# Pairing the last two gate blocks, requesting decay rows a step sooner, and taking group norm's roots on a whole row

## The chip, the cores and the metric

The kernel runs on one core of one Trainium2 chip. The metric is the device time of one execution in microseconds (us), as the median of the runs shown. A core has five engines that run side by side and wait for each other by semaphores: PE (TensorE, matrix products), DVE (VectorE), ACT (ScalarE), POOL (GpSimd) and SP (SyncE, which here only issues transfers). POOL also issues transfers, in the order of its own program.

## The reference

One decoder layer on 1024 tokens of width 1024. The part that matters here:

```python
hn = rms_norm(h, norm_mix_g)
za, zb, zc, xbc, dt_raw, g_raw = split(hn @ w_in)      # one projection feeds everything
ya = gmlp_mixer(za, ...)
yb = rg_lru_mixer(zb, ...)
yc = ssd_mixer(zc, xbc, dt_raw, ...)
gates = sigmoid(g_raw.reshape(..., 3, 1024) + b_gate)  # 24 blocks of 128 columns
merged = sum(gates[k] * (y_k @ w_branch_k) for k in range(3))
h = h + merged @ w_out
# ... then the MLP and a last norm

# inside ssd_mixer, in chunks of 128 tokens, 4 groups of 4 heads:
#   decay[l, s] = exp(acs[l] - acs[s])      (one row acs per chunk and head)
#   y = y_diag(decay) + exp(acs) * (C @ state) + x * d_skip
#   y = y * silu(z)
#   y = y * rsqrt(mean(y*y over the 256 columns of the group) + eps) * norm_g
```

## The kernel before, in words

Everything is computed in float32 split into a high and a low part, so that a product of two matrices is three products (high·high, high·low, low·high). Channels lie on the partitions and tokens on the columns.

**Units.** The projection is worked off in *units* of 128 output columns (`one_unit`, `product` L549): 48 matmuls (8 blocks of the inner dimension, 3 parts, 2 halves of 512 tokens) into one PSUM tile `ps` of 1024 columns. Two such tiles exist. After each unit its `post` function reads `ps`, and `step()` then lets every pending generator (`later(...)`) run to its next `yield`. So each `yield` is worth one unit of PE time, and a generator says in which unit's shadow its work is meant to lie. A scheduler then orders the instructions of each engine; every engine runs its own in order.

**The order of the units.** Four rounds, one for each SSD group g: b, c, x0, x1, z0, z1 (`ssd_units`), then two LRU heads with an x unit and a gate unit each (`lru_units`). Then eight GMLP units (`gmlp_unit`), then two single gate units (`gate_unit` L873, blocks 6 and 7 of branch 1), each a full unit of 48 matmuls. The other 22 gate blocks are computed after that as 11 *pairs* (`GatePair` L926): two blocks of 128 columns by 1024 tokens as a 2x2 block product with seven products in place of eight (`seventh` L472), each 12 matmuls of 512 columns, 84 for a pair. Pairs need sums of quarters of the normed input (`x_forms` L884: T1, T2, T4 and the third, written back over X at its end), which are prepared by steps under the GMLP units; the first pair's weights are prepared by `first_pair` (L978).

**The SSD stages** (`ssd_stages` L649) of a round have ten steps. The token halves 0 and 1 go through `rows_in` (L658, rows of the decays, 128 copies), `s1_` (L664, transposes, C·B products, decay matrices E), `s2_` (L697, chunk states `pv`), `s3_` (L722, y) , `roots_` (L743) and `s4_` (L749, norm and store). `s2_` begins with the requests for the tiles `er` (L701): four transfers on POOL's queue that copy rows of exp(acs) from DRAM to 64 partitions each. `s3_` multiplies by `er` on DVE (L735), straight out of the PSUM tiles `yo` that PE has just written, adds `yi` (L736), the skip (L737), and z (L738); then ACT squares (L740) and POOL adds the two squares (L741).

**The roots before.** `roots_` sums the squares over the partitions with four products by a single column of ones (L746), which leaves four columns of 128 numbers; `rsqrt_cols` (L115) takes the inverse roots of these four columns with three small DVE instructions and twelve small POOL instructions. `s4_` spreads them over the partitions with four products by the identity (L753) into a PSUM tile that two DVE instructions read (L756).

**Shared tiles.** PSUM tiles of 512 columns (`aux`, four of them) serve the transposes, C·B, chunk states, yo, yi, root sums and the LRU's gate products (L815). Tiles of 512 columns in SBUF (`half_`, sixteen) serve xdt, xw, pv, er, squares and the LRU's temporaries. A tile is given out anew when its last reader is done, so a late reader delays whatever takes the tile next.

**The order on POOL** is one queue for small arithmetic, for the transfers `wl` (L527, which make the low part of the next units' weights), for `yb_d`/`yc_d`/`ya_d` stores and for the requests of decay rows.

Of the kernel before, what the change touches and what calls it, by code (L numbers as in the profile page):

```python
# [8 lines left out]
F32 = mybir.dt.float32  # L9
# [3 lines left out]
ALU = mybir.AluOpType  # L13
# [23 lines left out]
def trunk_kernel(ctx: ExitStack, tc: tile.TileContext, x, norm_mix_g, w_in, b_gate, gmlp_ln_g, gmlp_ln_b,  # L37
# [37 lines left out]
    def half_(shape=(P, HF), dt=F32):  # L75
        return halfp.tile(list(shape), dt, tag="half", name=nm("h"))
# [208 lines left out]
    with tc.manual_schedule():  # L285
# [24 lines left out]
        nc.gpsimd.affine_select(out=tri, in_=ones, pattern=[[1, P]], compare_op=ALU.is_ge, fill=0.0,  # L310
                                base=0, channel_multiplier=-1)
        g2c = base.tile([P, 2 * KD], F32, name="g2c")
        groot = base.tile([P, 8], F32, name="groot")
        ss, rs = sm(NCH, "ss"), sm(NCH, "rsx")
        v2[NCH - 1] = act()

# [332 lines left out]
    def ssd_stages(g, S):  # L649
        Bf, Cf, Xf = S["b"], S["c"], (S["x0"], S["x1"])  # L650
        hs = slice(4 * g, 4 * g + 4)
        Bt = act((P, NCH, P))
        xdt, xw, E, cb, pv, er, sq = {}, {}, {}, {}, {}, {}, {}

        def tok(c):
            return slice(c * P, (c + 1) * P)

        def rows_in(half):  # L658
            for q in (2 * half, 2 * half + 1):
                e = E[q] = act((P, 2, 4, P))  # L660
                for cc in range(2):
                    nc.gpsimd.dma_start(out=e[:, cc], in_=acs_v[0, 2 * q + cc, hs, :].partition_broadcast(P))

        def s1_(half):  # L664
            for q in (2 * half, 2 * half + 1):
                ps = aux()
                for cc in range(2):
                    for j in range(2):
                        o = cc * 256 + j * P
                        nc.tensor.transpose(out=ps[:, o:o + P], in_=Xf[j][:, tok(2 * q + cc)], identity=ident)  # L670
                ev = ps.rearrange("p (c h d) -> p c h d", c=2, h=4)
                xdt[q], xw[q] = half_((P, 2, 4, 64)), half_((P, 2, 4, 64))
                tt(out=xdt[q], in0=ev, in1=dt[:, 2 * q:2 * q + 2, hs].unsqueeze(3).to_broadcast([P, 2, 4, 64]), op=ALU.mult)
                tt(out=xw[q], in0=ev, in1=w2[:, 2 * q:2 * q + 2, hs].unsqueeze(3).to_broadcast([P, 2, 4, 64]), op=ALU.mult)
            ps = aux()
            for i in range(4):
                nc.tensor.transpose(out=ps[:, tok(i)], in_=Bf[:, tok(half * 4 + i)], identity=ident)
            actv(Bt[:, half * 4:half * 4 + 4, :], ps.rearrange("p (c n) -> p c n", c=4), AF.Copy)
            cb[half] = aux()
            for i in range(4):  # L680
                c = half * 4 + i
                mm(cb[half][:, tok(i)], Bf[:, tok(c)], Cf[:, tok(c)], start=True, stop=True)

            cbm = half_((P, 4, P))
            tt(out=cbm, in0=cb[half].rearrange("p (c l) -> p c l", c=4), in1=tri.unsqueeze(1).to_broadcast([P, 4, P]), op=ALU.mult)
            for q in (2 * half, 2 * half + 1):
                e = E[q]
                for cc in range(2):
                    for h in range(4):
                        col = (2 * q + cc) * 16 + 4 * g + h  # L690
                        actv(e[:, cc, h, :], e[:, cc, h, :], AF.Relu, scale=-1.0, bias=acs[:, col:col + 1])
                actv(e, e, AF.Exp, scale=-1.0)
                for cc in range(2):
                    i = (2 * q + cc) % 4
                    tt(out=e[:, cc], in0=e[:, cc], in1=cbm[:, i].unsqueeze(1).to_broadcast([P, 4, P]), op=ALU.mult)

        def s2_(half):  # L697
            for j in range(2):
                t = er[half, j] = half_((P, 4, P))
                for h in range(2):  # L700
                    nc.gpsimd.dma_start(out=t[64 * h:64 * h + 64], in_=acs_v[1, half * 4:half * 4 + 4, 4 * g + 2 * j + h, :].partition_broadcast(64))  # L701
            for q in (2 * half, 2 * half + 1):
                if q == 0:
                    pv[0] = half_((P, 2, 256))
                    nc.gpsimd.memset(pv[0][:, 0, :], 0.0)
                st = aux()
                for cc in range(2):
                    mm(st[:, cc * 256:cc * 256 + 256], Bt[:, 2 * q + cc, :], xw[q][:, cc].rearrange("p h d -> p (h d)"), start=True, stop=True)
                for cc in range(2):
                    c = 2 * q + cc  # L710
                    if c == NCH - 1:
                        continue
                    if cc == 1:
                        pv[q + 1] = half_((P, 2, 256))
                    dst = pv[(c + 1) // 2][:, (c + 1) % 2, :]
                    for h in range(4):
                        col = c * 16 + 4 * g + h
                        o = slice(h * 64, h * 64 + 64)
                        stt(out=dst[:, o], in0=pv[q][:, cc, o], scalar=etot[:, col:col + 1],
                            in1=st[:, cc * 256 + h * 64:cc * 256 + h * 64 + 64], op0=ALU.mult, op1=ALU.add)  # L720

        def s3_(half):  # L722
            tk = hsl(half)
            for j in range(2):
                yo, yi = aux(), aux()
                for i in range(4):
                    c = half * 4 + i
                    mm(yo[:, tok(i)], pv[c // 2][:, c % 2, j * P:(j + 1) * P], Cf[:, tok(c)], start=True, stop=True)
                for i in range(4):
                    c = half * 4 + i  # L730
                    for h in range(2):
                        mm(yi[64 * h:64 * h + 64, tok(i)], xdt[c // 2][:, c % 2, 2 * j + h, :], E[c // 2][:, c % 2, 2 * j + h, :], start=True, stop=True)
                y = er[half, j].rearrange("p c l -> p (c l)")
                Z = S["z", j]
                tt(out=y, in0=yo, in1=y, op=ALU.mult)  # L735
                tt(out=y, in0=yi, in1=y, op=ALU.add)  # L736
                stt(out=y, in0=Xf[j][:, tk], scalar=dcol[:, 2 * g + j:2 * g + j + 1], in1=y, op0=ALU.mult, op1=ALU.add)  # L737
                tt(out=Z[:, tk], in0=y, in1=Z[:, tk], op=ALU.mult)  # L738
                sq[half, j] = half_()
                actv(sq[half, j], Z[:, tk], AF.Square)  # L740
            nc.gpsimd.tensor_tensor(out=sq[half, 0], in0=sq[half, 0], in1=sq[half, 1], op=ALU.add)  # L741

        def roots_(half):  # L743
            vs = aux()
            for i in range(4):
                mm(vs[:, i:i + 1], sq[half, 0][:, tok(i)], ones[:, :1], start=True, stop=True)  # L746
            rsqrt_cols(groot[:, 4 * half:4 * half + 4], vs[:, :4], 1.0 / 256, 4.0 * EPS)

        def s4_(half):  # L749
            tk = hsl(half)  # L750
            rb = aux()
            for i in range(4):
                mm(rb[:, tok(i)], groot[:, 4 * half + i:4 * half + i + 1].to_broadcast([P, P]), ident, start=True, stop=True)  # L753
            for j in range(2):
                Z = S["z", j]
                stt(out=Z[:, tk], in0=Z[:, tk], scalar=va[:, SNG + 2 * g + j:SNG + 2 * g + j + 1], in1=rb, op0=ALU.mult, op1=ALU.mult)  # L756
                nc.gpsimd.dma_start(out=yd["c"][2 * g + j][:, tk], in_=Z[:, tk])

        rows_in(0)
        yield  # L760
        s1_(0)
        yield
        s2_(0)
        yield
        s3_(0)
        rows_in(1)
        yield
        s1_(1)
        roots_(0)
        yield  # L770
        s2_(1)
        s4_(0)
        yield
        s3_(1)
        yield
        yield
        roots_(1)
        yield
        s4_(1)


# [65 lines left out]
    def gmlp_unit(g):  # L847
        def stages(u2):
            if g == 0:
                later(x_forms())  # L850
            elif g == 7:
                later(first_pair())
            yield
            vg = v_of.pop(g)
# [15 lines left out]

        unit_in(C_U + g * P, post)

    def gate_unit(br, e):  # L873
        def post(ps):
            t = act()
            actv(t, ps, AF.Tanh, scale=0.5, bias=vh[:, BG + br * 8 + e:BG + br * 8 + e + 1])
            nc.gpsimd.dma_start(out=gd[br][e], in_=t)
        unit_in(C_G + br * D + e * P, post)


    XF = {n: [[X.rhs(part, 4 * kh + kk, th) for kk in range(4)] for part in range(2)]
          for n, kh, th in (("B11", 0, 0), ("B21", 1, 0), ("B22", 1, 1), ("T3", 0, 1))}

    def x_forms():  # L884
        yield
        third = []
        for n in ("T1", "T2", "T4"):
            XF[n] = [[None] * 4, [None] * 4]
# [83 lines left out]
            self.gate(self.o1[:, hsl(1)], self.o1[:, hsl(1)], 1)  # L972
            nc.gpsimd.dma_start(out=gd[self.br][self.e + 1], in_=self.o1)

    pairs = [(1, e) for e in range(0, 6, 2)] + [(br, e) for br in (0, 2) for e in range(0, KD, 2)]
    cur = []

    def first_pair():  # L978
# [6 lines left out]
        yield  # L985
        z.w.cast12()

    gates = [(1, 6), (1, 7)]

    def some_gates(n):  # L990
        for i in range(n):
            gate_unit(*gates.pop(0))

    for r in range(4):
        ssd_units(r)
# [1 line left out]
        lru_units(2 * r + 1)  # L997
    for g in range(8):
        gmlp_unit(g)
    some_gates(2)  # L1000

    ahead(AHEAD)
    v_block(2, wv2)
# [624 lines left out]
```

## Time and profile before

| | us |
|---|---|
| median of 3 runs | 2039.29 (2033.38 to 2045.07) |
| the profiled execution's own time | 2037.77 |
| its span | 2036.1 |
| PE busy | 1973.0 (97%) |
| DVE busy | 1166.0 (57%) |
| ACT busy | 917.6 (45%) |
| POOL busy | 354.4 (17%) |
| four SSD/LRU rounds, about 165 to 712 us of the span | 140 each |
| GMLP and gate units, to about 815 us | 103 |
| eleven gate pairs, to about 1027 us | 212 |

The span counts from the first to the last instruction on the core; the profiled execution's own time is 1.7 us longer. In a timeline row the columns are the start, the duration, engine, line, operation, tiles (written <- read), shape and how many instructions the row merges; in square brackets stands the idle time of the engine just before the row and what ended it. Matmuls are pipelined and their ends are modelled, so starts are the safer reading. A float32 matmul that is not split is recorded as two.

### The profile page before, as it was taken

The page shows a single profiled execution, that of the slowest core. Times are in us where ns is not written, and L with a number is a line of the kernel's source. Part 1 is how long each engine was busy: PE and PEld are TensorE (multiplying, and loading weights), DVE is VectorE, ACT ScalarE, POOL GpSimd, SP SyncE. Part 2 cuts the span into 40 slices and gives each one's busy share as a digit, 9 for nine tenths or more (in the row PEclk, how much of TensorE's full clock was granted, in tenths as well). Part 3 has the DMA queues.
Part 4 walks back from the last instruction along what each step waited for, and adds up shares of the span by engine and source line. Part 5 has one row for each costly group of instructions (what it writes and reads, how often), then busy time and mean ns, then how long its engine had stood idle before and what let it go on. Part 6 is the DMA issues. An engine that isn't in the chain of part 4 may idle for free.

```text
span 2036.1 us, 24175 instructions
## 1 busy us (share of the span) xinstructions
PE 1973.0 (97%) x9280; PEld 1649.8 (81%) x9280; DVE 1166.0 (57%) x1768; ACT 917.6 (45%) x1348; POOL 354.4 (17%) x508
## 2 busy tenths in 40 slices
PE   8999999999999999999999999999899999999996
PEld 7998878788788788788878888787688887888885
DVE  5486655655655566544333213336766557787787
ACT  6434555556546433444443222236555555253243
POOL 4112322332432443000000220000111111000000
PEclk8999999999999999999999999999999999999998
DMA  4256447436455475333397665421544438644532
GB/s 156 67 155 127 104 105 153 95 96 138 93 120 124 104 177 154 114 114 109 116 324 194 176 147 144 160 89 51 167 135 161 160 131 305 211 130 144 185 107 92
DMA packets 215175, 286.59 MB, mean 141 GB/s; under 512 B 12580, under 2 KB 150004, under 8 KB 215060
## 3 DMA queue, kind: packets, MB, share of 16 engines
q1 hardware_dynamic: 175636, 144.91, 23.8%
q0 software_dynamic: 33488, 118.64, 22.7%
q10 hardware_dynamic: 5936, 21.51, 3.2%
q8 instruction: 73, 1.20, 0.2%
q14 instruction: 42, 0.34, 0.1%
HBM read 178.97 MB, written 67.24 MB: 121 GB/s over the span
## 4 chain that ended last, share of the span: by engine, by line
PE 77%; DVE 10%; DMA 4%; ACT 4%; POOL 3%; issue 2%; SPq 0%; DVEq 0%; POOLq 0%; ACTq 0%
PE ps L554 33%; PE aux L477 30%; PE gps L477 5%; PE aux L257 3%; DMA h<-acs_d 2%; PE aux L1158 2%; PE aux L815 1%; DVE rsq_q L111 1%; ACT a L1199 1%; PE aux L859 1%; DVE a L830 1%; DMA raw<-in_w_branch_c_dram 1%; DMA wl<-raw 1%; ACT a L132 1%; DVE a L133 1%
## 5 line engine op out<-in xcount | busy, mean ns | idle before, releaser
L554 PE MATMUL ps<-xn,wh 128*128 128x512 f32 x1600 | 434.4, 392 | 0.0
L554 PEld LDWEIGHTS ps<-xn,wh 128*128 128x128 f32 x1600 | 298.9, 188 | 61.4 <-issue 0.7
L554 PE MATMUL ps<-xn,wl 128*128 128x512 f32 x800 | 246.7, 389 | 0.0
L525 ACT ACTIVATE wh<-raw 128x1024 fp32r<-128x1024 f32 x74 | 78.2, 1056 | 275.2 <-PE ps L554 247.9
L477 PE MATMUL aux<-a,b 128*128 128x512 f32 x864 | 197.3, 389 | 0.0
L477 PEld LDWEIGHTS aux<-a,b 128*128 128x128 f32 x864 | 162.2, 188 | 33.7
L554 PEld LDWEIGHTS ps<-xn,wl 128*128 128x128 f32 x800 | 150.5, 188 | 31.7
L477 PE MATMUL aux<-b,wt 128*128 128x512 f32 x672 | 156.9, 389 | 0.0
L477 PEld LDWEIGHTS aux<-b,wt 128*128 128x128 f32 x672 | 126.1, 188 | 26.2
L527 POOL DMA_DIRECT2D wl<-raw x74 | 66.0, 891 | 403.9 <-ACT wl L526 292.3
L477 PE MATMUL aux<-b,b 128*128 128x512 f32 x480 | 110.6, 389 | 0.0
L1380 DVE TENSOR_TENSOR a<-aux,a 128x512 f32<-128x512 f32 x112 | 76.9, 687 | 50.5 <-PE aux L477 50.5
L477 PEld LDWEIGHTS aux<-b,b 128*128 128x128 f32 x480 | 90.1, 188 | 18.7
L1053 DVE SCALAR_TENSOR_TENSOR a<-a,ps 128x1024 f32<-128x1024 f32 x22 | 26.8, 1220 | 136.4 <-PE ps L554 123.6
L133 DVE TENSOR_TENSOR wt<-a,wt 128x1024 fp32r<-128x1024 f32 x50 | 61.3, 1226 | 69.1 <-ACT wt L132 69.1
L133 DVE TENSOR_TENSOR a<-a,a 128x1024 fp32r<-128x1024 f32 (+1 forms) x64 | 63.8, 1004 | 52.4 <-ACT a L132 52.3
L132 ACT ACTIVATE b<-wt 128x1024 fp32r<-128x1024 f32 x60 | 61.8, 1053 | 70.1 <-DMA wt<-u_d 51.2
L554 PE MATMUL ps<-c,wh 128*128 128x512 f32 x320 | 85.9, 390 | 0.5 <-DVE c L133 0.5
L477 PE MATMUL aux<-a,wt 128*128 128x512 f32 x336 | 78.7, 390 | 3.4 <-ACT a L1257 3.4
L132 ACT ACTIVATE a<-a 128x1024 fp32r<-128x1024 f32 (+1 forms) x64 | 55.1, 879 | 56.5 <-DVE a L1332 43.8
L526 ACT ACTIVATE wl<-wh 128x1024 fp32r<-128x1024 f32 x74 | 77.8, 1052 | 0.8
L477 PEld LDWEIGHTS aux<-a,wt 128*128 128x128 f32 x336 | 62.9, 188 | 17.2 <-ACT a L1257 4.2
(330 smaller groups left out, 3662.1 us busy)
## 6 DMA issues: line engine op xcount, KB each, us to landing
wl<-raw POOLq DMA_DIRECT2D x74, 512.0 KB, 5.3
wt<-u_d SPq DMA_DIRECT2D x54, 512.0 KB
raw<-in_w_in_dram SPq DMA_DIRECT2D x50, 512.0 KB
u_d<-a POOLq DMA_DIRECT2D x48, 512.0 KB, 5.4
g_d<-a POOLq DMA_DIRECT2D x24, 512.0 KB, 2.9
a<-g_d ACTq DMA_DIRECT2D x22, 512.0 KB
rt<-in_w_mlp_up_dram SPq DMA_DIRECT2D x17, 512.0 KB
a<-acs_d POOLq DMA_DIRECT2D x32, 256.0 KB, 7.6
```

Of the source, the lines that this page charges most:

```text
L111: stt(out=q, in0=r, scalar=nh, in1=r, op0=ALU.mult, op1=ALU.mult)
L132: actv(dst_hi, src, AF.Copy)
L133: (eng or nc.vector).tensor_tensor(out=dst_lo, in0=src, in1=dst_hi.bitcast(F32), op=ALU.subtract)
L257: mm(ps[:, :nt], X.tok(a, k, c), wk[k][w], start=(k == 0 and i == 0), stop=(k == KD - 1 and i == 2))
L477: mm(ps, lhs[l][kk], rhs[r][kk], start=(new and n == 0), stop=(n == 11), skip_group_check=not new)
L525: actv(hi, raw, AF.Copy)
L526: actv(lo, hi.bitcast(F32), AF.Copy, scale=-1.0)
L527: nc.gpsimd.dma_start(out=lo, in_=raw, accum_op=ALU.add)
L554: mm(ps[:, hsl(h)], w[wi][:, k, :], a.rhs(ai, k, h), start=(n == 0), stop=(n == 3 * KD - 1))
L1053: stt(out=t, in0=t, scalar=1.0, in1=ps, op0=ALU.add, op1=ALU.mult)
L1158: mm(ps, M.tok(a, k, c), wo[nb][k][w], start=(k == 0 and a + w == 0), stop=(k == KD - 1 and a == 1))
L1380: tt(out=h, in0=ps, in1=h, op=ALU.add)
```

## The change

Three edits:

1. **Gate blocks.** The two single gate units go; blocks 6 and 7 of branch 1 become a twelfth pair. `x_forms` and `first_pair` start one and two units sooner, to stand in the same place before the pairs.
2. **Decay rows.** The four requests for `er` move from the start of `s2_` to the start of `s1_`, one step sooner.
3. **Roots.** `roots_` and its calls go. `s4_` now sums the squares with one product by a full matrix of ones, so that every partition holds the sum for its column (512 columns). ACT takes the square root, DVE the reciprocal, and four more DVE instructions make one Newton step; the final two DVE instructions then read an SBUF tile in place of PSUM. `s4_(0)` runs in the step of `s1_(1)`, one step sooner than before; `s4_(1)` comes two steps after `s3_(1)`, one step sooner than before.

```diff
@@ constants
-        groot = base.tile([P, 8], F32, name="groot")
+        eps4 = base.tile([P, 1], F32, name="eps4")
+        nc.vector.memset(eps4, 4.0 * EPS)
@@ ssd_stages
         def s1_(half):
+            for j in range(2):
+                t = er[half, j] = half_((P, 4, P))
+                for h in range(2):
+                    nc.gpsimd.dma_start(out=t[64 * h:64 * h + 64], in_=acs_v[1, half * 4:half * 4 + 4, 4 * g + 2 * j + h, :].partition_broadcast(64))
             for q in (2 * half, 2 * half + 1):
...
         def s2_(half):
-            for j in range(2):
-                t = er[half, j] = half_((P, 4, P))
-                for h in range(2):
-                    nc.gpsimd.dma_start(out=t[64 * h:64 * h + 64], in_=acs_v[1, half * 4:half * 4 + 4, 4 * g + 2 * j + h, :].partition_broadcast(64))
             for q in (2 * half, 2 * half + 1):
...
-        def roots_(half):
-            vs = aux()
-            for i in range(4):
-                mm(vs[:, i:i + 1], sq[half, 0][:, tok(i)], ones[:, :1], start=True, stop=True)
-            rsqrt_cols(groot[:, 4 * half:4 * half + 4], vs[:, :4], 1.0 / 256, 4.0 * EPS)
-
         def s4_(half):
             tk = hsl(half)
-            rb = aux()
-            for i in range(4):
-                mm(rb[:, tok(i)], groot[:, 4 * half + i:4 * half + i + 1].to_broadcast([P, P]), ident, start=True, stop=True)
+            vs = aux()
+            mm(vs, ones, sq[half, 0], start=True, stop=True)
+            r, q = half_(), half_()
+            actv(r, vs, AF.Sqrt, scale=1.0 / 256, bias=eps4)
+            nc.vector.reciprocal(out=r, in_=r)
+            tt(out=q, in0=r, in1=r, op=ALU.mult)
+            stt(out=q, in0=vs, scalar=256 * 4.0 * EPS, in1=q, op0=ALU.add, op1=ALU.mult)
+            ts(out=q, in0=q, scalar1=-0.5 / 256, scalar2=1.5, op0=ALU.mult, op1=ALU.add)
+            tt(out=r, in0=r, in1=q, op=ALU.mult)
             for j in range(2):
                 Z = S["z", j]
-                stt(out=Z[:, tk], in0=Z[:, tk], scalar=va[:, SNG + ...], in1=rb, op0=ALU.mult, op1=ALU.mult)
+                stt(out=Z[:, tk], in0=Z[:, tk], scalar=va[:, SNG + ...], in1=r, op0=ALU.mult, op1=ALU.mult)
                 nc.gpsimd.dma_start(out=yd["c"][2 * g + j][:, tk], in_=Z[:, tk])
...
         rows_in(1)
         yield
         s1_(1)
-        roots_(0)
+        s4_(0)
         yield
         s2_(1)
-        s4_(0)
         yield
         s3_(1)
         yield
-        yield
-        roots_(1)
         yield
         s4_(1)
@@ gmlp_unit
-            elif g == 7:
+            elif g == 5:
                 later(first_pair())
@@ gate units
-    def gate_unit(br, e): ...
     def x_forms():
-        yield
         third = []
@@ pairs
-    pairs = [(1, e) for e in range(0, 6, 2)] + [(br, e) for br in (0, 2) for e in range(0, KD, 2)]
+    pairs = [(br, e) for br in (1, 0, 2) for e in range(0, KD, 2)]
...
-    some_gates(2)
```

Two places in the order of the instructions. On POOL, in the first round, from the weights' transfer under the first LRU unit up to the second pair of stores; `h ... <-acs_d` is an `er` request, `wl` a weights' transfer, `yc_d` the stores of half 0, `yb_d` an LRU store. Before:

```order
L829 TENSOR_TENSOR h_2394<-h_2394,h_2388 128x512
L832 TENSOR_TENSOR a_2279<-a_2361,a_2279 128x1024
L833 DMA yb_d<-a_2279 128x1024
L527 DMA wl_2521<-raw_2518 128x1024
L757 DMA yc_d<-a_1953 128x512
L757 DMA yc_d<-a_2065 128x512
L701 DMA h_2484<-acs_d 64x4x128 x2
L701 DMA h_2487<-acs_d 64x4x128 x2
```

After (here `er` is requested at L669, L742 is POOL's sum of the squares, L758 the stores, L824 and L827 POOL's part of the LRU):

```order
L528 DMA wl_2227<-raw_2224 128x1024
L669 DMA h_2286<-acs_d 64x4x128
L742 TENSOR_TENSOR h_2195<-h_2195,h_2215 128x512
L669 DMA h_2286<-acs_d 64x4x128
L669 DMA h_2289<-acs_d 64x4x128 x2
L528 DMA wl_2409<-raw_2406 128x1024
L758 DMA yc_d<-a_1954 128x512
L758 DMA yc_d<-a_2072 128x512
L824 TENSOR_SCALAR h_2372<-h_2372 128x512
L824 TENSOR_SCALAR h_2394<-h_2394 128x512
L827 TENSOR_TENSOR h_2370<-h_2370,h_2364 128x512
```

The four requests stood behind the first LRU head's last product, two stores and a weights' transfer; now they stand around the sum of the squares, ahead of all of that head's POOL work.

On DVE, in the step of `s1_(1)` of the first round: L695 (after: L700) makes the decay matrices, L828, L824, L825 and L830 (after: L826, L822, L823 and L828) are the LRU head's gates and scan, `lw` its weights, `etot` the chunk states. Before:

```order
L685 TENSOR_TENSOR h_2314<-aux_2309,tri 128x512
L118 TENSOR_SCALAR rsqn_r_2344<-aux_2338 128x4
L695 TENSOR_TENSOR a_2217<-a_2217,h_2314 128x512 x2
L695 TENSOR_TENSOR a_2220<-a_2220,h_2314 128x512 x2
L119 TENSOR_SCALAR rsqn_v_2343<-rsqn_r_2344 128x4
L828 SCALAR_TENSOR_TENSOR h_2372<-h_2372,a_2156 128x512
L120 TENSOR_SCALAR rsqn_r_2344<-rsqn_r_2344 128x4
L824 SCALAR_TENSOR_TENSOR h_2374<-h_2374,h_2366 128x512
```

After:

```order
L690 TENSOR_TENSOR h_2321<-aux_2316,tri 128x512
L700 TENSOR_TENSOR a_2218<-a_2218,h_2321 128x512 x2
L700 TENSOR_TENSOR a_2221<-a_2221,h_2321 128x512 x2
L750 RECIPROCAL h_2347<-h_2347 128x512
L751 TENSOR_TENSOR h_2348<-h_2347 128x512
L752 SCALAR_TENSOR_TENSOR h_2348<-aux_2345,h_2348 128x512
L753 TENSOR_SCALAR h_2348<-h_2348 128x512
L754 TENSOR_TENSOR h_2347<-h_2347,h_2348 128x512
L757 SCALAR_TENSOR_TENSOR a_1954<-a_1954,va,h_2347 128x512
L757 SCALAR_TENSOR_TENSOR a_2072<-a_2072,va,h_2347 128x512
L826 SCALAR_TENSOR_TENSOR h_2370<-h_2370,a_2157 128x512
L822 SCALAR_TENSOR_TENSOR h_2372<-h_2372,h_2364 128x512
```

Seven instructions on 512 columns now stand between the decay matrices and the LRU's gates, where two on four columns stood; the two that apply the norm come here from the next step. On ACT the square root stands, between two loads of its function table, ahead of the LRU's four gate functions. On PE the fourth of the LRU's gate products, which followed the third directly, now stands 28 matmuls of the unit behind it.

More of the change, by code (lines that the diff above doesn't have):

```diff
@@ L741, in s3_ @@
             nc.gpsimd.tensor_tensor(out=sq[half, 0], in0=sq[half, 0], in1=sq[half, 1], op=ALU.add)
-        def roots_(half):
-            vs = aux()
-            for i in range(4):
-                mm(vs[:, i:i + 1], sq[half, 0][:, tok(i)], ones[:, :1], start=True, stop=True)
-            rsqrt_cols(groot[:, 4 * half:4 * half + 4], vs[:, :4], 1.0 / 256, 4.0 * EPS)
         def s4_(half):
             tk = hsl(half)
-            rb = aux()
-            for i in range(4):
-                mm(rb[:, tok(i)], groot[:, 4 * half + i:4 * half + i + 1].to_broadcast([P, P]), ident, start=True, stop=True)
+            vs = aux()
[7 more added lines that the diff above has]
+            tt(out=r, in0=r, in1=q, op=ALU.mult)
             for j in range(2):
                 Z = S["z", j]
-                stt(out=Z[:, tk], in0=Z[:, tk], scalar=va[:, SNG + 2 * g + j:SNG + 2 * g + j + 1], in1=rb, op0=ALU.mult, op1=ALU.mult)
+                stt(out=Z[:, tk], in0=Z[:, tk], scalar=va[:, SNG + 2 * g + j:SNG + 2 * g + j + 1], in1=r, op0=ALU.mult, op1=ALU.mult)
                 nc.gpsimd.dma_start(out=yd["c"][2 * g + j][:, tk], in_=Z[:, tk])
@@ L871, in gmlp_unit @@
         unit_in(C_U + g * P, post)
[L873 to L878, printed above, removed]
     XF = {n: [[X.rhs(part, 4 * kh + kk, th) for kk in range(4)] for part in range(2)]
@@ L986, in first_pair @@
         z.w.cast12()
[L988 to L992, printed above, removed]
     for r in range(4):
```

## The prediction

> **What bounds the kernel now.** I read the page first, then PE's waits, then PE's and DVE's timelines around the longest wait.
>
> ```profile
> PE 1973.0 (97%) x9280; PEld 1649.8 (81%) x9280; DVE 1166.0 (57%) x1768; ACT 917.6 (45%) x1348; POOL 354.4 (17%) x508
> ```
> ```profile
> PE aux L815 <- DVE h L735: 13.4, 4, 3.8
> PE aux L815 <- DVE h L736: 0.9, 2, 0.7
> ```
>
> PE sets the time: it is busy for 97% of 2036.1 us. So a change can gain in two ways only, by fewer PE instructions or by fewer PE waits. Its waits (second view: who, for whom, us in total, times, longest) are led by one place that comes once in each round: the LRU gate products (L815) wait until DVE has read a PSUM tile (L735). PE's timeline of the first round and of the last (start, duration, ..., idle time before) shows what that costs:
>
> ```profile
> 258.20 1.09 PE L732 MATMUL aux<-a,h 128*64 128x128 f32 x16
> 262.80 1.40 PE L815 MATMUL aux<-h,lw 128*128 128x512 f32 x3 [3.51 <-DVE h L735]
> 264.44 3.27 PE L815 MATMUL aux<-h,lw 128*128 128x512 f32 x9 [0.24 <-DVE h L736]
> 267.54 1.09 PE L554 MATMUL ps<-xn,wh 128*128 128x512 f32 x4
> ...
> 679.24 1.09 PE L732 MATMUL aux<-a,h 128*64 128x128 f32 x16
> 689.28 1.30 PE L554 MATMUL ps<-xn,wh 128*128 128x512 f32 x4
> ```
> ```profile
> 261.96 0.69 DVE L735 TENSOR_TENSOR h<-aux,h 128x512 f32<-128x512 f32 x1 [7.13 <-DMA h<-acs_d]
> ```
> ```profile
> 249.59 1.45 POOL yc_d L757 x2
> 251.05 0.48 POOL h L701
> 251.53 10.31 DMA h<-acs_d
> ```
>
> From the start of the last products of y (L732) to the next unit (L554) pass 9.34 us in the first round and 10.04 in the fourth. The work in it is 1.0 us for L732 and twelve products of 0.227 (below), 3.7 in all. So about 6.0 us a round are lost, 24 in four rounds; the waits alone (14.3) are less, because the products behind the wait run slow: nine in 3.27 us, where 2.04 are due. The cause stands on DVE: it sat idle for 7.13 us until the `er` rows landed at 261.9. The chain (third fence) tells why so late: POOL issued their requests at 251, behind two stores, and they took 10.3 us.
>
> **Gate blocks.** One unit has 48 matmuls, one of the pair's products 12:
>
> ```profile
> 740.41 10.90 PE ps L554 x48
> 846.69 2.72 PE aux L477 x12
> ```
>
> Two units are 21.8 us, a pair's seven products 19.04, so PE gains 2.8. Both kinds are on PE's path whole. The pair's ACT and DVE work (L132, L133, L501 to L506) lies under its products as in the eleven pairs there are.
>
> **The cover at the end.** The units were also cover. Without the last two, the matmuls of the last two GMLP groups, the forms and the first pair's splits meet right behind the last unit. Before, the first pair's first products stood like this:
>
> ```profile
> 817.27 2.88 PE L477 MATMUL aux<-xn,wt 128*128 128x512 f32 x12
> 821.09 0.73 PE L477 MATMUL aux<-h,wt 128*128 128x512 f32 x2 [0.94 <-ACT wt L132]
> 822.35 2.58 PE L477 MATMUL aux<-h,wt 128*128 128x512 f32 x10 [0.53 <-DVE wt L133]
> 824.77 2.88 PE L477 MATMUL gps<-h,wt 128*128 128x512 f32 x12
> ```
> ```profile
> 808.89 4.56 DVE L133 TENSOR_TENSOR xn<-a,xn 128x1024 fp32r<-128x1024 f32 x2
> 816.91 1.22 DVE L133 TENSOR_TENSOR a<-a,a 128x1024 fp32r<-128x1024 f32 x1 [3.45 <-ACT a L132]
> ```
> ```profile
> 807.93 3.31 POOL L862 TENSOR_TENSOR a<-a,a 128x1024 f32<-128x1024 f32 x1 [1.96 <-DVE a L860]
> ```
>
> From 817.27 to 824.77 two products take 7.5 us in place of 5.44: 2.1 lost today. After the change I count DVE's work behind the last unit by the new order: from its end DVE still has about 2 forms, 3 splits, a gelu and the first pair's sums ahead of the two GMLP instructions that give back the PSUM tile of the second product; at 0.6 us for 512 columns and 1.15 for 1024 (the rows above) that is 9.4 us, while PE has 3.6 (two GMLP groups) and 2.7 (first product) to do. So PE waits 3.1 there and 0.4 for the next split: 1.4 more than today. A split that runs beside POOL's L862 loses about 2.2 (second and third fence: two take 4.56, one alone 1.22), and two of these can meet: up to 4.6 more than today, and nothing more if the forms end sooner. I take 3.5, since such meetings were there before, too.
>
> **The roots, on PE.** They cost, per half, these two groups; the product over 512 columns isn't in the trace, its nearest row is the float32 product over 256 (four products, eight records):
>
> ```profile
> 289.49 0.79 PE aux L746 x8
> 301.32 0.89 PE aux L753 x8
> 197.25 1.73 PE aux L708 x8
> ```
>
> 1.73 by 4 is 0.43 for 256 columns, so 0.86 for 512. 0.79 and 0.89 go and 0.86 comes: 0.8 gained per half, eight halves, 6.5 us, all on PE's path.
>
> **The roots, on DVE.** The two reciprocals there are, and the rows for the rest:
>
> ```profile
> L222 DVE RECIPROCAL a<-a 128x128 f32<-128x128 f32 x1 | 1.0, 954 | 0.0
> L222 DVE RECIPROCAL a<-a 128x8 f32<-128x8 f32 x1 | 0.2, 202 | 0.0
> L1013 DVE TENSOR_SCALAR a<-a,bmv,lrs 128x1024 f32<-128x1024 f32 x8 | 6.5, 812 | 0.3
> ```
> ```profile
> 230.88 2.50 DVE L695 TENSOR_TENSOR a<-a,h 128x512 f32<-128x512 f32 x4
> 247.47 0.74 DVE L756 SCALAR_TENSOR_TENSOR a<-a,va,aux 128x512 f32<-128x512 f32 x1
> 253.22 1.62 DVE L719 SCALAR_TENSOR_TENSOR h<-h,etot,aux 128x64 f32<-128x64 f32 x8
> ```
> ```profile
> 236.65 1.28 ACT L827 ACT_TABLE_LOAD   x1
> ```
> ```profile
> 255.10 1.05 PE L728 MATMUL aux<-a,h 128*128 128x128 f32 x8
> ```
>
> 120 columns more cost 752 ns, 6.3 ns a column: 3.4 us for 512. Then two products of 0.6 (four of L695 take 2.50), one of 0.7, and 0.4 for L753 (half of L1013): 5.7 us, and 1.4 for the two L757, which only move. In the order of the new program this stands from 233.3 (end of L695) to 240.4, ahead of the LRU's gates. Two places can make PE wait for it:
>
> - The fourth gate product takes the PSUM tile of the root sums, which L752 gives back at 233.3 + 3.4 + 0.6 + 0.7 = 238.0. PE comes there at 227.0 + 0.86 + 9 gate matmuls and 37 of the unit at 0.227 = 238.3. So it just doesn't wait, with 0.3 us to spare; each microsecond more on DVE would be one on PE, four times.
> - The chunk states. Behind 240.4 stand 4.8 us of gates and states, a wait for POOL's product to about 246, two scans (3.5), a convolution (3.6), two splits with ACT's part (1.9) and eight L719 (1.6): 256.6, against 254.84 before (253.22 and 1.62). It is only 1.8 late, not 7, because POOL's twelve small instructions, which held the scans before, are gone. PE comes to y at 254.2, 0.9 sooner than at 255.10, and needs the third chunk's state about 0.8 us later. So a wait of about 1 us a round stays, 4 in all, from 0 (states in time) to 2.5 a round (all 1.8 late plus POOL's collisions).
>
> ACT's root needs the table twice (1.28 each): it ends near 231, 2 us before DVE can use it, and the gates' functions come 2.6 us later than now, still ahead of DVE's 240. In the other half the chain stands between convolutions, where a unit's 10.9 us hold 4.8 of DVE work: about 6 more leave the PSUM tile free in time. Price there: 0, and 1 to 2 us for each of four halves if that cover fails.
>
> [...]
>
> **The decay rows.** POOL's order now has the requests around its sum of the squares; the first needs the tile that L738 last read, so POOL issues them near 217 and 222 to 225. With 10.3 us they land by about 236, 20 us before the products of y. Behind them in POOL's queue stand a weights' transfer that is wanted two units later and the stores; both have slack. So the wait of DVE goes. What is late next is the chunk states, priced above. The slow products behind the wait should go, too, since the gate products of the step before, without a wait ahead of them, ran at 0.227. [...]
>
> **The sum.** Against the profiled execution's 2037.8: 24 for the waits gained, 4 of it kept, 6.5 for the roots, 2.8 for the pair, and 3.5 lost at the end of the units: 25.8 less, 2012. The median shown is 1.5 above that execution: 2039.3 less 25.8 is 2013.5; I say 2013.
>
> **Rivals.**
> - *The wait comes back on DVE* (12%). The chain of seven is 2 to 3 us slower than I make it, so that both the fourth gate product and the states come late, some 3 us a round, with cold products behind it. Against it: DVE idles for 7.13 us just there. For it: 0.3 us of margin. 2012 plus 12 gives 2024 to 2026.
> [...]
> - *The rows aren't sooner* (6%). If POOL's request waits for a tile of the sixteen that comes free late, the 24 stay and only 6.5 and 2.8 less 3.5 are gained: about 2033, within the measurement's grain. Against it: the order puts the requests ahead of POOL's LRU work, and L738 is long done.
> - *Slower: DVE becomes the bound of the rounds* (4%). The eight chains hold 5.7 us each, and if none of it is hidden, 46 come onto the path against 33 gained and 3.5 lost: about 2055. It decides where DVE has under 6 us of idle time in the step; against it, DVE is busy for only 57% of the span.
>
> **How the numbers follow.** The forecast has 72%, its own range 2004 (no wait left, nothing lost at the end) to 2021 (2.5 us a round, 4.6 at the end). With the first rival's lower half and the second the range is 2003 to 2027, which leaves out some 18%. A measurement of this kernel tells apart about 0.5%, 10 us: the three runs before span 11.7. Faster by more, under 2029, are the forecast, the first rival and the second: 0.90. Same: the third, 0.06. Slower: 0.04.
>
> **What would show it.** In the profile after: L735's successor waits for PE, not for `acs_d`; under 5 us from the last product of y to the next unit's start (with twelve gate products 3.7); the root's product 0.9 us; RECIPROCAL 3.4 us; 84 matmuls for the twelfth pair. I am wrong if PE waits over 2 us a round for the chunk states or the fourth gate product, if the first pair's start costs over 7 us, or if the reciprocal is well over 4 us.

## The result, and the profile after

The changed kernel takes 2026.82 us, the median of six runs (2023.37 to 2028.56), where the kernel before took 2040.2 in the runs beside it: a ratio of 0.9933 (95% interval 0.9912 to 0.9954), 13.4 us less. The direction was forecast, and the time lies at the upper end of the range (2003 to 2027), but only half of the 26 us came. The profiled execution took 2023.37 us, span 2021.7, so between the two traces lie 14.4 us.

The page after, its first line: PE has lost 13.7 us of work and is as full as before, DVE has gained 53.6.

```profile
PE 1959.3 (97%) x9156; PEld 1633.8 (81%) x9156; DVE 1219.6 (60%) x1796; ACT 944.5 (47%) x1377; POOL 326.6 (16%) x410
```

PE's waits (who, for whom, us in total, times, longest). The gate products (L815, now L813) have left the list. In their place the products of y (L729) wait for the chunk states (L720), four times, and there is a new wait of a pair's product for a GMLP instruction (L858):

```profile
PE aux L729 <- DVE h L720: 8.1, 4, 2.2
...
PE aux L478 <- DVE a L858: 4.5, 1, 4.5
```

PE's timeline at the products of y, in the first round and in the second:

```profile
254.01 0.60 PE L729 MATMUL aux<-a,h 128*128 128x128 f32 x4
...
257.21 0.49 PE L729 MATMUL aux<-a,h 128*128 128x128 f32 x2 [2.23 <-DVE h L720]
...
260.77 0.73 PE L555 MATMUL ps<-xn,wh 128*128 128x512 f32 x2
261.34 2.92 PE L813 MATMUL aux<-h,lw 128*128 128x512 f32 x12
...
389.35 0.60 PE L729 MATMUL aux<-a,h 128*128 128x128 f32 x4
...
392.27 0.77 PE L729 MATMUL aux<-a,h 128*128 128x128 f32 x2 [1.95 <-DVE h L720]
392.97 1.55 PE L733 MATMUL aux<-a,h 128*64 128x128 f32 x12
...
397.40 0.74 PE L555 MATMUL ps<-xn,wh 128*128 128x512 f32 x2
```

From the first product of y to the next unit pass 6.76 us in the first round and 8.05, 8.01 and 7.98 in the others. Without a wait it is 4.12 (so in the other token half of every round), so 14.3 us are lost in four rounds. 8.1 are the waits; most of the rest is products that run slow behind them. In the second round the work behind the wait takes 5.13 us (392.27 to 397.40), in the first 3.56 (257.21 to 260.77).

The chain of waits, followed back from there, lies on DVE from 229.77 on, but for two instructions of POOL, one of ACT and short gaps (start, duration, what):

```profile
230.49 2.50 DVE a L700 x4
232.98 3.27 DVE h L750
...
245.66 1.27 POOL h L827
246.95 2.31 DVE a L828
...
254.82 0.64 ACT h L132
255.48 1.29 DVE h L133 x2
256.77 0.39 DVE h L720 x2
257.17 0.04 issue
257.21 0.49 PE aux L729 x2
```

The reciprocal that the third edit added stands near its start, and at its end PE's product starts 0.04 us behind the state that it needs.

The start of the pairs, on PE. From the first product (775.63) to the fourth (791.10) pass 15.47 us where three products are 8.16:

```profile
772.14 3.73 PE L857 MATMUL aux<-wT,a 128*128 128x128 f32 x32
775.63 2.98 PE L478 MATMUL gps<-xn,wt 128*128 128x512 f32 x12
783.09 5.42 PE L478 MATMUL aux<-xn,wt 128*128 128x512 f32 x12 [4.48 <-DVE a L858]
788.35 2.92 PE L478 MATMUL aux<-h,wt 128*128 128x512 f32 x12
791.10 2.88 PE L478 MATMUL gps<-h,wt 128*128 128x512 f32 x12
```

### The profile page after: what moved, and what is told of

The parts are those of the page before. It is cut to its first block, busy times and chain, and to the rows that moved or that the text cites. A ratio compares the mean times of both kernels' runs of the same rounds, so it can differ in the third digit from the quotient of the medians.

```text
span 2021.7 us, 23919 instructions
## 1 busy us (share of the span) xinstructions
PE 1959.3 (97%) x9156; PEld 1633.8 (81%) x9156; DVE 1219.6 (60%) x1796; ACT 944.5 (47%) x1377; POOL 326.6 (16%) x410
## 4 chain that ended last, share of the span: by engine, by line
PE 78%; DVE 13%; ACT 3%; DMA 3%; issue 2%; POOL 0%; SPq 0%; DVEq 0%; ACTq 0%; POOLq 0%
PE ps L555 32%; PE aux L478 30%; PE gps L478 6%; PE aux L257 3%; PE aux L1142 2%; DVE a L578 1%; PE aux L729 1%; PE aux L733 1%; PE aux L813 1%; DVE rsq_q L111 1%; DMA raw<-in_w_branch_c_dram 1%; DMA a<-in_x_dram 1%; ACT a L1183 1%; DVE a L828 1%; DVE h L750 1%
## 5 line engine op out<-in xcount | busy, mean ns | idle before, releaser
L555 PE MATMUL ps<-xn,wh 128*128 128x512 f32 x1536 | 418.3, 392 | 0.0
L555 PEld LDWEIGHTS ps<-xn,wh 128*128 128x128 f32 x1536 | 286.9, 188 | 61.1 <-issue 2.8
L555 PE MATMUL ps<-xn,wl 128*128 128x512 f32 x768 | 236.6, 389 | 0.0
L555 PEld LDWEIGHTS ps<-xn,wl 128*128 128x128 f32 x768 | 144.2, 188 | 30.1
```

Source lines behind the costliest of these rows:

```text
L555: mm(ps[:, hsl(h)], w[wi][:, k, :], a.rhs(ai, k, h), start=(n == 0), stop=(n == 3 * KD - 1))
```

## The experiments

The theory from the two traces: the late `er` rows were the whole of the old loss at the products of y, and their edit removes it; the new roots put 7.4 us on DVE ahead of the chunk states and so bring a second loss at the same place; the pairs' edit trades 2.8 us of products for a longer gap. The rivals: the states are late for reasons of their own, or the edits collide elsewhere. All experiments were timed in five rounds beside the kernel before (2041.0 to 2041.3 us).

| kernel | median us | ratio to before, 95% interval |
|---|---|---|
| second edit alone (rows) | 2016.04 | 0.9878 (0.9861 to 0.9896) |
| third edit alone (roots) | 2031.79 | 0.9954 (0.9939 to 0.9969) |
| first edit alone (pair) | 2040.39 | 0.9995 (0.9986 to 1.0005) |
| rows and roots, no pair | 2020.66 | 0.9899 (0.9885 to 0.9912) |
| all three (the change) | 2026.82 | 0.9933 (0.9912 to 0.9954) |
| all, reciprocal of half 0 twice | 2031.66 | 0.9948 (0.9935 to 0.9961) |
| all, no Newton step in half 0 | 2012.66 | 0.9864 (0.9848 to 0.9880) |
| all, root of half 0 behind y | 2016.28 | 0.9881 (0.9861 to 0.9901) |
| the same, no pair | 2011.33 | 0.9848 (0.9835 to 0.9861) |
| root behind y, first pair sooner | 2014.39 | 0.9866 (0.9852 to 0.9879) |
| the same, sums of X sooner too | 2006.03 | 0.9832 (0.9817 to 0.9847) |

### Each edit alone

The rows alone: the kernel before with the four requests moved from `s2_` to `s1_`, as in the diff above.

> The kernel before with the second edit alone: the requests for the er rows one step sooner; the old roots and the two single gate units stay. Theory: the 24 us at the products of y come from the late rows and from nothing else, and the 14.3 us that the changed kernel still loses there come from the new roots' chain on DVE, which makes the chunk states late. Without the new roots the states are ready at about 254.8 of the first round, as before, so the loss goes nearly whole: 24 less 0 to 5, 2016 to 2021 us, no wait of PE for a chunk state over 1 us. Rival: what is late behind the rows is late for reasons of its own (the LRU's work on DVE and POOL), whatever the roots do: then only about 9 us are gained, as in the rounds of the changed kernel without the roots' own PE time, 2030 to 2032 us, and PE waits about 2 us a round for the states here too.

2016.04 us, 25.0 less. PE's timeline at the products of y in the first round:

```profile
254.05 1.05 PE L728 MATMUL aux<-a,h 128*128 128x128 f32 x8
...
258.17 3.02 PE L815 MATMUL aux<-h,lw 128*128 128x512 f32 x12
261.02 1.07 PE L554 MATMUL ps<-xn,wh 128*128 128x512 f32 x4
```

6.97 us from the first product of y to the next unit, in every round, where 12.44 to 13.14 stood: no wait and no slow product. The last states end ahead of PE's first product:

```profile
252.16 1.62 DVE L719 SCALAR_TENSOR_TENSOR h<-h,etot,aux 128x64 f32<-128x64 f32 x8
```

The smallest of the three edits, by itself, beats the whole change by 10 us. That the states come late for reasons of their own is out.

The roots alone: the third edit's lines only.

> The kernel before with the third edit alone: root over a whole row, the er rows still requested in the later step. Theory: PE gains the 6.0 us of the shorter root products (0.75 in eight halves), and the chain on DVE, which makes the chunk states 2 us late, costs nothing as long as the er rows are later still: 2033 to 2037 us, with the wait for the rows still there in each round. Rival: the chain on DVE costs PE time by itself, here too (the states come late first and the rows then follow): no gain or a loss, 2040 to 2046 us.

2031.79 us, 9.2 less, somewhat more than expected (the interval reaches from 6.3 to 12.5). In the traces the two spans differ by 5.8 (2036.1 and 2030.3), which is what the root products give. The wait for the rows is still there, somewhat shorter (the multiplication by `er`, L735 before, is L736 in this kernel), and the states come 0.7 us late at most:

```profile
PE aux L813 <- DVE h L736: 12.5, 8, 3.4
...
PE aux L729 <- DVE h L720: 2.6, 4, 0.7
```

So the roots cost PE little as long as the rows come later still.

The pair alone: the first edit's lines only.

> The kernel before with the first edit alone: a twelfth pair in place of two single gate units. Theory: 2.8 us less for PE's products, but PE's losses between the last unit and the first pair grow by 5.2 us, as they did in the changed kernel (7.3 where 2.1 stood): 2041 to 2044 us, with one wait of 4 to 5 us for a GMLP instruction of DVE and slow products behind it. Rival, the prediction's own sum: the losses grow by 1.4 to 3.5 us, net 1.4 less to 0.7 more: 2038 to 2041 us, and the wait is 3 us.

2040.39 us, 0.6 less (interval 2.9 less to 1.0 more). The median fell to the rival's side, the wait to the theory's:

```profile
790.20 2.98 PE L477 MATMUL gps<-xn,wt 128*128 128x512 f32 x12
797.65 4.61 PE L477 MATMUL aux<-xn,wt 128*128 128x512 f32 x12 [4.48 <-DVE a L860]
...
804.86 1.52 PE L477 MATMUL gps<-h,wt 128*128 128x512 f32 x6
```

14.66 us from the first product to the fourth, 6.5 lost where the kernel before lost 2.1. The products' 2.7 us are more than given back there; the medians don't show the difference.

### The roots on top of the rows

The changed kernel without its first edit.

> The changed kernel without its first edit: er rows sooner and the new roots, but the two single gate units stay. It stands beside the run of the second edit alone (2016.0 us), from which it differs by the new roots only. Theory: the roots' chain on DVE makes the chunk states late as soon as the er rows don't hide it; PE gets 6.0 us shorter root products and 14.3 us of waits and slow products, so that an edit which gains 9 us by itself here loses about 8: 2023 to 2027 us, PE waiting about 2 us a round for the states. Rival: the loss comes from the meeting with the pairs' edit (tiles, weights' transfers), not from the roots: 2008 to 2012 us here.

2020.66 us: the roots, which gain 9.2 alone, cost 4.6 on top of the rows. The waits for the states are as in the changed kernel, without any twelfth pair:

```profile
PE aux L729 <- DVE h L720: 8.2, 4, 2.2
```

The sign is the theory's, the size was expected larger (7 to 11), and the time lies outside both forecasts. The intervals of the two ratios overlap a little (0.9885 and up here, up to 0.9896 with the rows alone), so the sign rests on the waits in the trace as much as on the medians. The products of y take 8.34, 8.06, 8.04 and 8.06 us in its trace, 16 lost, of which the roots' own 6 must be taken; trace and medians agree within some 5 us only.

The root of the first half moved behind the products of y:

```diff
         s1_(1)
-        s4_(0)
         yield
         s2_(1)
         yield
         s3_(1)
         yield
+        s4_(0)
         yield
         s4_(1)
```

> The changed kernel with the root and norm of the first token half moved from the step of s1_(1) to the step behind s3_(1): the same work, but DVE's chain of seven now stands behind the chunk states and the products of y. Theory: the states are no longer late, the 14 us that PE loses at the products of y go nearly whole, and the chain lies under the next units: 2026.8 less 10 to 14, 2012 to 2017 us. Rival: the states are late for other reasons (POOL's product, the convolution): 2025 to 2029 us, and PE still waits about 2 us a round. A second rival: the chain then delays what it stands ahead of, the convolutions of the next x unit, and PE waits for a PSUM tile there: above 2020 us with the wait at another line.

2016.28 us, 10.5 less than the change. DVE's last states and PE's products of y in the first round:

```profile
249.73 1.62 DVE L720 SCALAR_TENSOR_TENSOR h<-h,etot,aux 128x64 f32<-128x64 f32 x8
```
```profile
253.19 1.05 PE L729 MATMUL aux<-a,h 128*128 128x128 f32 x8
...
257.31 3.02 PE L813 MATMUL aux<-h,lw 128*128 128x512 f32 x12
260.16 1.07 PE L555 MATMUL ps<-xn,wh 128*128 128x512 f32 x4
```

The states end at 251.35 instead of 258.30, 1.8 us ahead of PE, and the products of y and the gates take 6.97 us in every round, as with the rows alone. At another place in DVE's order the same instructions cost PE nothing at the products of y. Of the 14.3 us lost there 10.5 came back in the medians; this kernel is one of four that lose more behind the pairs (below, under what stays open).

The reciprocal of half 0 done twice:

```diff
+            if half == 0:
+                nc.vector.reciprocal(out=q, in_=r)
             nc.vector.reciprocal(out=r, in_=r)
```

> The changed kernel with the reciprocal of the first token half done twice (the first result goes to a tile that is overwritten): 3.34 us more on DVE ahead of the chunk states, four times, nothing else. Theory: DVE's chain stands on PE's path, each microsecond of it is one of PE's: 13.4 us more and up to 2 us a round of slow products behind the longer wait, 2038 to 2048 us; part of the wait may move to the fourth gate product, whose tile the chain gives back 0.2 us ahead of PE. Rival: the states are late for POOL's product, the convolution or the transfers: 2026 to 2030 us.

2031.66 us, 4.8 more, a third of the 13.4 that the theory asked for and outside both forecasts. The two ratios' intervals overlap (0.9935 to 0.9961 and 0.9912 to 0.9954), so the size is uncertain. The trace shows another order: the scheduler put one of the LRU's gates between the two reciprocals and the others among the instructions behind them, so that POOL had its part sooner and DVE's wait for it (1.68 us in the change) is gone.

```profile
232.55 3.35 DVE L751 RECIPROCAL h<-h 128x512 f32<-128x512 f32 x1
235.81 0.63 DVE L828 SCALAR_TENSOR_TENSOR h<-h,a 128x512 f32<-128x512 f32 x1
236.35 3.34 DVE L752 RECIPROCAL h<-h 128x512 f32<-128x512 f32 x1
...
257.58 1.62 DVE L720 SCALAR_TENSOR_TENSOR h<-h,etot,aux 128x64 f32<-128x64 f32 x8
```

The states end at 259.20, 0.9 us later, not 3.34. This run changed the order of DVE's work as well as its amount, so its small price says little on the chain as it stands in the change.

The Newton step of half 0 left out (its root is then that of the square root and the reciprocal alone):

```diff
+            if half == 1:
-            tt(out=q, in0=r, in1=r, op=ALU.mult)
+                tt(out=q, in0=r, in1=r, op=ALU.mult)
...
```

> The changed kernel with the four instructions of the Newton step left out for the first token half (the root there is that of the square root and the reciprocal alone): 2.5 us less on DVE ahead of the chunk states, in each round; the second half keeps them. Theory: the states are late by the chain's length, so PE's wait for them (2.0 to 2.2 us a round) falls under 0.5 and the slow products behind it go too: 10 to 14 us less, 2013 to 2017 us. Rival, after the doubled reciprocal cost only about half of its length: what DVE is given is taken up by idle time and by another order, and about half of the 10 us comes back: 2020 to 2023 us. If the chain had no part in it: 2025 to 2029 us.

2012.66 us, 14.2 less for 2.5 us of DVE work a round, ten in all: just past the theory's end. The states end at 254.90 in the first round, and PE's product of y (253.74) doesn't wait for them in any round:

```profile
253.29 1.61 DVE L720 SCALAR_TENSOR_TENSOR h<-h,etot,aux 128x64 f32<-128x64 f32 x8
```
```profile
253.74 1.32 PE L729 MATMUL aux<-a,h 128*128 128x128 f32 x8
```

More than the ten came back: the slow products went with the wait. The states came 3.4 us sooner for 2.5 us of work, since here, too, gates moved ahead of the norm and shortened the wait for POOL (0.69 us left of 1.68).

### The pair, with the rest in order

The kernel with the root behind y, without the twelfth pair.

> The same without the first edit, and with the root of the first half behind the products of y. Against the second edit alone (2016.0 us) PE's root products are 6.0 us shorter and no wait takes their place. Theory: 2009 to 2012 us. Against the same kernel with the twelfth pair (2016.3 us): if the pair's edit costs the 2.4 us of its rows (2.8 gained, 5.2 lost), the pair-free kernel is at 2013 to 2015. Rival: the 6 us do not show because something behind the pairs takes them back (the transfers that the branch products wait for): 2015 to 2018 us.

2011.33 us: 4.7 less than the rows alone by the medians, where 6.0 were expected from the shorter root products. The traces agree only in part: the fourth product of the first pair starts 6.7 us sooner (792.63 for 799.37), but the span ends only 2.1 sooner (2009.7 for 2011.8), so that some of the gain is given back behind the pairs, as the rival had it. And 5.0 less than the same kernel with the twelfth pair; 6.1 was the same difference between the change and its run without the pair. So the pair's edit costs about 5 us here, though nothing alone; each interval reaches 2 to 4 us to either side, and the rows (5.2 lost, 2.7 gained) account for 2.5 of it.

The first pair begun one GMLP unit sooner, in the kernel with the root behind y and the pair:

```diff
-            elif g == 5:
+            elif g == 4:
                 later(first_pair())
```

> The kernel with the root behind the products of y and all 24 gate blocks in pairs (2016.3 us), with the first pair's splits and sums begun one GMLP unit sooner. Theory: what PE loses between the last unit and the pairs (7.5 us in that kernel's trace) is DVE's work of the first pair that stands ahead of the GMLP instruction that gives the PSUM tile back; 5 to 6 us of it move under a unit, the wait of 4.5 us falls under 1 and the slow products go: 4 to 6 us less, 2010 to 2013 us. Rival: DVE is full there whatever the order (the forms alone fill the last two units): 2015 to 2017 us, with a wait of 3 us or more left.

2014.39 us, 1.9 less, between the two forecasts and inside the noise. The gap shrank only in part:

```profile
760.97 2.98 PE L478 MATMUL gps<-xn,wt 128*128 128x512 f32 x12
766.06 4.23 PE L478 MATMUL aux<-xn,wt 128*128 128x512 f32 x12 [2.12 <-DVE a L858]
...
774.74 3.01 PE L478 MATMUL gps<-h,wt 128*128 128x512 f32 x12 [1.31 <-ACT a L931]
```

13.77 us where 8.16 are due. So the sums of X were moved as well. The `yield` that goes stands in a loop that runs twice, so the sums start up to one unit sooner and the later ones come two units sooner; only their last splits, which overwrite X, must wait for the last unit:

```diff
             tt(out=t3, in0=t3, in1=e, op=ALU.add)
-            yield
             tt(out=d, in0=quarter(0, 0, 0), in1=t3, op=ALU.add)
...
             yield
+        yield
+        yield
         assert not queue
```

> The kernel with the root behind the products of y, all blocks in pairs and the first pair one unit sooner (2014.4 us; PE still lost 5.6 us between the last unit and the pairs), with the sums of X for the pairs two units sooner as well, all but the last splits, which must wait for the last unit. Theory: what is left of the loss is DVE's sums and splits of X; about 9 us of them move under earlier units and PE loses what it lost with the two units as cover, 2 us: 2009 to 2012 us, the twelfth pair then no dearer than the two units (2011.3 us without it). Rival: DVE's idle time under the GMLP units is used up and the work comes out at the same place: 2013 to 2016 us.

2006.03 us, 8.4 less, more than forecast, and the fastest of all: ratio to before 0.9832 (0.9817 to 0.9847). PE passes into the pairs without a wait:

```profile
760.29 2.98 PE L478 MATMUL gps<-xn,wt 128*128 128x512 f32 x12
...
768.55 2.88 PE L478 MATMUL gps<-h,wt 128*128 128x512 f32 x12
```

8.26 us for 8.16 of work. With the preparation sooner the kernel with the twelfth pair is 5.3 us faster than the pair-free one by the medians, where it was 5.0 slower; the intervals of the two ratios overlap (0.9817 to 0.9847 and 0.9835 to 0.9861). Not all of that is the pair's: its products save 2.7, and the pair-free kernel still loses 2.1 at the same place, since its preparation was not moved.

## Why the prediction was half right

The terms, as predicted and as the two traces have them:

| term | predicted us | in the traces |
|---|---|---|
| waits for the rows, with the slow products | -24 | -24.1 |
| what stays for the chunk states | +4 | +14.3 |
| root products on PE | -6.5 | -6.0 |
| 84 products for 96 | -2.8 | -2.7 |
| the start of the pairs | +3.5 | +5.2 |
| sum | -25.8 | -13.3 |

The traces' numbers: from the first product of y to the next unit stood 12.44, 12.63, 12.73 and 13.14 us before, 6.97 each is what it takes without a wait, which makes 23.1, and 1.0 for slow products of the unit behind it in the last two rounds; the 14.3 are shown above; the two old groups for the roots take 0.81 us each from start to start and the new product 0.87, in eight halves; 96 products of 0.227 less 84; and 7.3 us lost at the pairs' start less 2.1. The remaining 1.1 of the 14.4 lies elsewhere in the span and was not traced.

**The rows** went as forecast: the requests are out of the way and no wait of DVE for `acs_d` is left; the second edit alone gives 25.0. **The root products** and **the pair's products** are the sizes that their rows gave: the full product by ones takes 0.86 us in the chain of waits, as worked out from the 256-column row, and the reciprocal 3.34 where its two rows gave 3.4. All eight reciprocals of the changed kernel lie between 3.34 and 3.35 us.

**The step that failed** is "So a wait of about 1 us a round stays, 4 in all". The mechanism was the right one, the size was 14.3. One of the signs that the prediction named against itself came true with it: PE waited over 2 us a round for the chunk states, if barely (8.1 in four rounds). Two things made the size. First, the sum along DVE ended at 256.6 and the states really ended at 258.30:

```profile
238.92 1.42 DVE L757 SCALAR_TENSOR_TENSOR a<-a,va,h 128x512 f32<-128x512 f32 x2
...
246.95 2.30 DVE L828 TENSOR_TENSOR_SCAN a<-h,h 128x512 f32<-128x512 f32 x1 [1.68 <-POOL h L827]
...
250.56 3.89 DVE L578 SCALAR_TENSOR_TENSOR a<-ps,va,a 128x1023 f32<-128x1023 f32 x3
255.48 1.29 DVE L133 TENSOR_TENSOR h<-a,h 128x512 fp32r<-128x512 f32 x2 [1.03 <-ACT h L132]
256.69 1.61 DVE L720 SCALAR_TENSOR_TENSOR h<-h,etot,aux 128x64 f32<-128x64 f32 x8
```

The chain of seven ended at 240.3 as forecast (240.4). Behind it POOL's product let the scan go at 246.95, not 246, the convolution took some 0.3 more and the splits with ACT's part 0.4 more: 1.7 us, each link a little. The wait was 2.0 to 2.2 us instead of 1.0. PE's product needs only the first two of the eight L720 (they end at 257.16, and it starts at 257.21), so by the prediction's own sum, with L720 from 255.0 and PE ready at 255.0, the wait would have been about 0.4; the 1.7 come on top of that. Second, the prediction's sum counts the wait alone and lets the products behind it run at full speed. They didn't:

```profile
257.00:261.00 4.00, 3.79 (x41) 3.21 (x42) 4.00 (x11) 3.97 (x4) 0.87 (x1) 1.00 0.51 90
...
392.20:397.50 5.30, 5.23 (x41) 4.38 (x41) 4.01 (x11) 3.97 (x4) 0.86 (x1) 0.68 0.65 126
...
783.00:788.30 5.30, 5.21 (x12) 4.13 (x13) 5.30 (x8) 0.98 (x2) 3.91 (x1) 0.50 0.52 146
```

These are windows of the changed kernel (length, busy time of PE, PEld, DVE, ACT and POOL, then the granted clock). After 2.23 us without work the clock stayed at 1.00 in the first round; after 1.95 it was 0.68 in the second, and after 1.96 also 0.68 in the third and fourth (528.85 to 534.15 and 665.46 to 670.76); after 4.48 it was 0.50. So waits of under 2 us were followed by the slower clock in three of four rounds. Against the first round that adds 1.5 to 1.6 us to each. Waits of the forecast length did go with full speed at other places: one of 0.94 us in the kernel before (821.09) and one of 1.06 us in the changed kernel (1699.92) were followed by a clock of 1.00 over 5 us. The wait that came was twice as long.

**The fourth gate product** did not wait: L752 gave its tile back at 237.69 (237.00 and 0.69) and PE came at 238.21; 238.0 and 238.3 had been worked out.

**The start of the pairs** cost 5.2 us more than before, above the 3.5 that the prediction took and above its upper end of 4.6; the loss there is 7.3 in all, and the prediction had named a cost of over 7 us as a sign of being wrong. The wait is 4.48 where 3.1 was counted, since DVE was through with the two GMLP instructions 10.9 us behind the last unit (772.14 to 783.09), not 9.4, and 2.5 us of slow product stand behind it. Part of the reason lies in the edit itself: two units went, and `x_forms` starts only one sooner, so that, unlike `first_pair`, it does not stand in the same place before the pairs. Its second set of sums starts 32.8 us ahead of the first product before (781.75 to 814.55) and 23.4 in the change (752.24 to 775.63):

```profile
781.75 1.22 DVE L902 TENSOR_TENSOR a<-xn,xn 128x1024 f32<-128x1024 f32 x1
```
```profile
752.24 1.22 DVE L892 TENSOR_TENSOR a<-xn,xn 128x1024 f32<-128x1024 f32 x1
```

In the fastest kernel, where PE passes into the pairs without a wait, it is 36.2 (724.08 to 760.29).

**The range and the rivals.** That 2026.8 lies inside the range is luck: the forecast's own range ended at 2021, and the rest up to 2027 was added for two rivals, more waiting on DVE and a slower reciprocal, neither of which came as described. No run shows the slower reciprocal's term: the rows of it over 512 columns have 3.34 or 3.35 us, under the forecast's 3.4. 2026.8 is nearest to "The wait comes back on DVE" (2024 to 2026, 12%). Its place and its slow products were there, but not its cause: the chain of seven was no slower than forecast, and only the states were late. It was given too little chance, because the forecast had 0.8 us between PE's coming and the need of the third state and counted a chain of eight links as if each were exact.

What stays open: behind the pairs, at the start of the branch products, the faster kernels lose some of what they gained. From the fourth product of the pair to the end the span has 1211 to 1212 us before, after and with the rows alone (with the extra pair taken off), 1213 to 1215 in the other runs but one (1212), and 1216 to 1218 in the four kernels with the root behind y. Nothing here tells whether that is their order or the time at which their transfers meet.

## What to carry to other kernels

When a wait goes, what stands second behind it sets the gain: follow the next releaser's whole chain on its engine, link by link, and if it ends within a few microseconds of the consumer, take the late end as the forecast, with slow products behind the wait (here 1.5 to 1.6 us of them at three of the four waits). Work that is off the bounding engine still has a place in its own engine's order: the same seven instructions cost 10 us more ahead of the chunk states than behind the products of y. And an instruction block that is removed from the bounding engine may have been the cover of a preparation; move all of the preparation sooner by at least as much (here the sums of X had moved by one unit where two went), and the removal can pay.

## What the runs showed of the hardware

In the changed kernel, the waits of TensorE for the chunk states of 1.95 and 1.96 us were followed by a granted clock of 0.68 over 5.3 us, in three of four rounds, while the one of 2.23 us in the first round left it at 1.00. In the run without the pair the first round's products ran slow, too: behind its wait of 2.24 us the ten records of L729 took 2.44 us from start to start (258.28 to 260.72), where the changed kernel took 1.32 in that round (258.43 to 259.75) and 1.92 in the second (394.45 to 396.37). The traces don't tell why the one wait was spared. A reciprocal over 512 columns took 3.34 us; the two rows of the kernel before, 202 ns for 8 columns and 954 for 128, differ by 6.3 ns a column, and from the second of them to 512 columns it is 6.2 ns a column.
